# First two tiles of an FFN half-step together, a third of the tokens at a time, and a table for the steps of the norm

## The chip, the cores and the metric

The kernel runs on one core of a Trainium2 chip, as one program. The metric is its device time in microseconds (us). PE is TensorE, DVE VectorE, ACT ScalarE, POOL GpSimd, and SP the queue that issues most DMAs. Each engine works through its own queue of instructions in the order in which the program puts them, and waits at an instruction until what it needs has been signalled.

## What is computed

A diffusion backbone of two layers over 512 latent tokens and 256 context tokens of width 1024, in fp32. Each layer is a half-step FFN, a token mixing (two groups of attention heads with rotary positions, one output projection), and another half-step FFN. The last half-step is for the latent tokens alone.

```python
def swiglu_half_step(x, g, mod, j, w_up, w_down):
    h = modulate(rms_norm(x, g), mod[..., j, :], mod[..., j + 1, :])
    gt, up = jnp.split(h @ w_up, 2, axis=-1)
    return x + MACARON_W * mod[..., j + 2, :] * ((jax.nn.silu(gt) * up) @ w_down)

def reference(...):
    for l in range(DEPTH):
        x = swiglu_half_step(x, norm_g[l, 0], mod_x, 0, w_ffn_up[l, 0], w_ffn_down[l, 0])
        h_ctx = swiglu_half_step(h_ctx, norm_g[l, 0], mod_c, 0, w_ffn_up[l, 0], w_ffn_down[l, 0])
        ...
        x = x + mod_x[..., 5, :] * (jnp.concatenate([out_a, out_b], axis=-1) @ w_out[l])
        ...
        x = swiglu_half_step(x, norm_g[l, 2], mod_x, 6, w_ffn_up[l, 1], w_ffn_down[l, 1])
    return x
```

rms_norm divides each token by the root of its mean square; mod_x and mod_c come from a product of the conditioning vector with a large matrix, w_ada. FFN(l,j) below is half-step j of layer l: FFN(0,0), mixing, FFN(0,1), FFN(1,0), mixing, FFN(1,1).

## The kernel before

Tokens lie along the free dimension, channels on the 128 partitions; x is eight tiles of 128 channels. An fp32 product is three matmuls of rounded halves (`mm3`, L536 to L538): high x high, high x low, low x high. So everything that PE multiplies is split first: an activation into xh (ACT, L502) and xl (DVE, L503), a piece of 512 weight columns into whi (ACT, L144) and wlo (DVE, L145). Raw weights and wlo share a ring of 15 buffers, whi has six.

A half-step has 22 tiles f of 128 hidden channels, in five groups. The first PLAIN[l,j] tiles are plain: gate and up, eight k-steps, 48 matmuls for each range of tokens. The others take seven Strassen products of 12 matmuls each, over half the tokens. These need sums of the inputs, which `combine` makes (L518 to L528) once all tokens are normed, and sums of the weights (DVE, L131).

The norm of a half-step's input is begun at the end of the step before it. While the last output tiles of a range of tokens come out (a residual, L756; a square on ACT, L463; its sum into acc on DVE, L464), `background` sets up a generator `norm` for each range that is through. With FULL tokens the ranges are thirds of 256 tokens (latent, latent, context); in FFN(1,1) two halves of the latent tokens. `tick` moves all waiting generators one step; it is called after each output tile, and after every second k-step of a plain tile. A generator's steps are:

- the **root**: `rstd`, small matmuls that sum acc over the partitions (L483), a scaling on DVE (L485, the tile st), a power on POOL (L486);
- the **spread**: two transposes on PE that lay st over all partitions (L492);
- the **multiplies** (L498), xh (L502) and xl (L503), eight tiles of each.

Before, the root came at a generator's second tick and the spread at its fifth, everywhere. `flush` moves a generator on until its range is ready, if its products come before that.

The first tile f=0 goes a third at a time, so that the first third's products can run while the others are normed; from f=1 on a tile takes all tokens at once, hence needs all thirds. In FFN(0,0) f=0 is made at the start, ahead of this code.

A dot product of w_ada with the conditioning vector (`ada`, L449, on DVE; its weights adaw come by DMA) is put in wherever a tile begins, behind the last xl or split at that point (`self.anchor`). The mixing starts with projections (L880 to L882) per third, and builds tables for the rotation on POOL (L863, L870) from a load on SP (`ropet`, L859).

A scheduler turns the program's order into one queue for each engine; what it moves is shown under the change.

Of the kernel before, what the change touches and what calls it, by code (L numbers as in the profile page):

```python
# [28 lines left out]
PLAIN = {(0, 0): 3, (0, 1): 3, (1, 0): 3, (1, 1): 2}  # L29
# [39 lines left out]
class Weights:  # L69


    def __init__(self, k):
# [42 lines left out]
    def prepare(self, upto):  # L115
        while self.split < min(upto, len(self.order)):
# [45 lines left out]


# [6 lines left out]
class Kern:  # L170
# [336 lines left out]
    def combine(self, l, j, streams):  # L507
# [7 lines left out]
        for k in range(4):  # L515
# [9 lines left out]
            for d in (k, k + 4):  # L525
# [4 lines left out]
                x[d] = low  # L530


    def mm3(self, o, wh, wl, h, l, first, last, more=False):
# [4 lines left out]
        mm(o, wl, h, start=False, stop=last, skip_group_check=more)  # L538

    def ffn(self, l, j, first, streams, then):  # L540
# [16 lines left out]
        def hidden():  # L557
            hh = self.fp.tile([P, T], F32R, tag="hh", name="hh", bufs=5)
            return hh, self.fp.tile([P, T], F32, tag="hl", name="hr", bufs=6)

        def parted(hh, hr):
# [9 lines left out]
        def plain(f, item):  # L571

            done = begun and f == 0
            strs = first if f == 0 and not done else streams
            if done:
                o = self.first
            else:
                o = [[self.bank()[:, :s1 - s0] for _, s0, s1 in strs] for _ in range(2)]
                for sel in [[i] for i in range(len(strs))] if f == 0 else [range(len(strs))]:
                    if f == 0:  # L580
                        self.flush(strs[sel[0]][1])
                    for k in range(KD):
                        for gu in range(2):
                            w = [z[:, k % 4 * P:k % 4 * P + P] for z in ws.ready((item, k // 4 * 2 + gu))]
                            for i in sel:
# [704 lines left out]
```

## Time and profile before

| | us |
|---|---|
| median of three runs | 2694.51 |
| lowest and highest run | 2690.70, 2695.86 |
| the profiled execution | 2696.01 |
| its span, first to last instruction | 2693.9 |
| PE busy in the span | 2605.4 |
| DVE busy | 2091.5 |
| ACT busy | 1286.3 |
| POOL busy | 151.0 |
| mean granted clock of PE | 0.985 |

The durations of the next section are from the profiled execution. Rows of the timeline give the start in the span, the busy time, the engine, the line, and the instruction, written as output<-inputs; "x8" behind a row is eight in a row, and the bracket says how long the engine was idle before it and what ended that. Rows of a stretch give, for each engine, busy us and the number of instructions, then PE's granted clock (1.00 is full speed), the DMA share and GB/s. Rows of waits give the engine and what it waited for, us in all, how often, and the longest. PEld is the loading of weights into PE.

### The profile page before, as it was taken

Reading aid. Unit: us, or ns where it says so; the run is one execution under the profiler, and the core shown is the slowest. Engines: PE = TensorE matmul, PEld = TensorE weight load, DVE = VectorE, ACT = ScalarE, POOL = GpSimd, SP = SyncE. Lnnn points to the kernel's source line nnn. Section 1 sums busy time; section 2 is a strip of 40 time slices with the busy share of each in tenths; the row PEclk is TensorE's granted clock in tenths of the full one; section 3 lists DMA queues with packets and bytes.
Section 4 is the critical chain, followed back from the end, with each engine's and each line's share of the span. In section 5 each row is a group of like instructions: output and inputs, shape, how many; then the busy total and the mean of one; then the engine's idle time right before and its main releaser. Section 6 shows DMA issues by size and latency. Waiting matters only on the chain. (4 is left out here: it accounts for less than half of the span.)

```text
span 2693.9 us, 47286 instructions
## 1 busy us (share of the span) xinstructions
PE 2605.4 (97%) x17078; PEld 2471.4 (92%) x17078; DVE 2091.5 (78%) x4198; ACT 1286.3 (48%) x2671; POOL 151.0 (6%) x255
## 2 busy tenths in 40 slices
PE   7999999999999989999999899999998999799999
PEld 5999999989999879999999799999998998789998
DVE  6988888777889698788666877676767779787776
ACT  5343343445777553343344533432435677545543
POOL 0000000033210000000000000000014110000000
PEclk9999999999999989999999899999998999899999
DMA  8656646444235537466434365466345335555553
GB/s 325 198 185 204 214 130 211 124 134 142 90 93 174 171 112 225 147 198 210 154 96 147 113 189 193 132 200 199 108 145 152 98 105 167 164 167 177 159 165 116
DMA packets 306153, 433.22 MB, mean 161 GB/s; under 512 B 31440, under 2 KB 177232, under 8 KB 304464
## 3 DMA queue, kind: packets, MB, share of 16 engines
q1 hardware_dynamic: 305920, 430.21, 50.8%
q8 instruction: 134, 2.20, 0.3%
q14 instruction: 99, 0.81, 0.1%
HBM read 344.90 MB, written 88.34 MB: 161 GB/s over the span
## 5 line engine op out<-in xcount | busy, mean ns | idle before, releaser
L144 ACT CAST whi<-wraw 128x512 fp32r<-128x512 f32 (+1 forms) x644 | 389.3, 611 | 721.3 <-PE b L537 615.7
L145 DVE TENSOR_TENSOR wlo<-wraw,whi 128x512 fp32r<-128x512 f32 (+1 forms) x644 | 425.9, 674 | 62.9 <-ACT whi L144 43.6
L537 PE MATMUL b<-xl,whi 128*128 128x384 f32 (+2 forms) x1420 | 452.0, 320 | 2.0 <-DVE xl L503 2.0
L538 PE MATMUL b<-xh,wlo 128*128 128x384 f32 (+2 forms) x1420 | 448.9, 320 | 3.3 <-DVE wlo L145 3.3
L536 PE MATMUL b<-xh,whi 128*128 128x384 f32 (+2 forms) x1420 | 447.6, 320 | 3.3 <-ACT xh L502 3.1
L537 PE MATMUL b<-hl,whi 128*128 128x512 f32 (+1 forms) x1292 | 432.1, 337 | 0.0
L538 PE MATMUL b<-hh,wlo 128*128 128x512 f32 (+1 forms) x1292 | 427.8, 336 | 0.0
L536 PE MATMUL b<-hh,whi 128*128 128x512 f32 (+1 forms) x1292 | 413.5, 337 | 0.0
L537 PE MATMUL b<-x,whi 128*128 128x384 f32 (+1 forms) x1232 | 395.6, 322 | 0.0
L536 PE MATMUL b<-sh,whi 128*128 128x384 f32 (+1 forms) x1232 | 394.1, 322 | 0.9 <-ACT whi L144 0.5
L538 PE MATMUL b<-sh,wlo 128*128 128x384 f32 (+1 forms) x1232 | 388.0, 321 | 0.0
L449 DVE CUSTOM_DVE_ANT_0 junk<-adaw,sc,bada 128x1024 bf16<-128x1024 f32 x224 | 286.8, 1280 | 8.2 <-DMA adaw<-in_w_ada 6.1
L537 PEld LDWEIGHTS b<-xl,whi 128*128 128x128 f32 x1420 | 273.6, 193 | 8.1 <-DVE xl L503 2.6
L538 PEld LDWEIGHTS b<-xh,wlo 128*128 128x128 f32 x1420 | 272.2, 192 | 8.6 <-DVE wlo L145 3.7
L536 PEld LDWEIGHTS b<-xh,whi 128*128 128x128 f32 x1420 | 271.2, 193 | 9.5 <-ACT xh L502 3.6
L144 ACT CAST whi<-wt 128x512 fp32r<-128x512 f32 x231 | 144.1, 624 | 261.7 <-PE b L537 220.4
L537 PEld LDWEIGHTS b<-hl,whi 128*128 128x128 f32 x1292 | 244.7, 189 | 24.8
L538 PEld LDWEIGHTS b<-hh,wlo 128*128 128x128 f32 x1292 | 244.3, 189 | 25.1
L536 PEld LDWEIGHTS b<-hh,whi 128*128 128x128 f32 x1292 | 241.2, 189 | 26.2
L880 PE MATMUL mm<-whi,xh 128*128 128x256 f32 x800 | 231.8, 291 | 10.1 <-ACT raw L892 4.1
L536 PEld LDWEIGHTS b<-sh,whi 128*128 128x128 f32 x1232 | 231.9, 188 | 3.0 <-ACT whi L144 1.7
L537 PEld LDWEIGHTS b<-x,whi 128*128 128x128 f32 x1232 | 232.1, 188 | 1.5
(159 smaller groups left out, 4858.7 us busy)
## 6 DMA issues: line engine op xcount, KB each, us to landing
wraw<-in_w_up SPq DMA_DIRECT2D x352, 256.0 KB
adaw<-in_w_ada SPq DMA_DIRECT2D x130, 512.0 KB
wraw<-in_w_down SPq DMA_DIRECT2D x160, 256.0 KB
xsp<-x SPq DMA_DIRECT2D x140, 256.0 KB
xsp<-x SPq DMA_DIRECT2D x184, 128.0 KB
xl<-xsp SPq DMA_DIRECT2D x80, 256.0 KB
xh<-xsp SPq DMA_DIRECT2D x80, 256.0 KB
wraw<-in_w_in SPq DMA_DIRECT2D x72, 256.0 KB
```

The source lines that it names most:

```text
L144: k.nc.scalar.copy(hi[:, :w], raw[:, :w])
L145: k.nc.vector.tensor_tensor(out=lo[:, :w], in0=raw[:, :w], in1=hi[:, :w].bitcast(F32), op=ALU.subtract)
L449: nc.vector.tensor_tensor_reduce(out=junk, in0=w, in1=self.sc[:, cond, :], scale=1.0, scalar=self.bada[:, l, n:n + 1], op0=ALU.mult, op1=A ...
L536: mm(o, wh, h, start=first, stop=False, skip_group_check=more)
L537: mm(o, wh, l, start=False, stop=False, skip_group_check=more)
L538: mm(o, wl, h, start=False, stop=last, skip_group_check=more)
L880: nc.tensor.matmul(o, self.xh[:, k, ts], wh, start=k == 0, stop=False)
```

## The change

Three things change.

1. `PLAIN[(1,1)]` goes from 2 to 3, so FFN(1,1) has a third plain tile and one Strassen tile less.
2. In FFN(0,1), (1,0) and (1,1), `plain_two` makes f=0 and f=1 together: for each range of tokens first f=0's products, then f=1's. The weights of f=1 are now needed through all ranges; their high halves go into buffers for hidden activations (tag hh, five of them). `combine` becomes a generator: of its four steps, two come behind f=0's last range and two behind f=1's. FFN(0,0) goes on as it was.
3. `TICKS` gives the ticks of root and spread: for each range, by what comes next. "ffn" is a half-step in thirds, "mix" a mixing, "lat" the two halves of FFN(1,1). They were 2 and 5 for all.

```diff
-PLAIN = {(0, 0): 3, (0, 1): 3, (1, 0): 3, (1, 1): 2}
+PLAIN = {(0, 0): 3, (0, 1): 3, (1, 0): 3, (1, 1): 3}
...
+            if gi == 0 and (l, j) != (0, 0):
+                ws.guest.add(up[1])
...
-        hi = k.wsp.tile([P, PW], F32R, tag="whi", name="whi")
+        hi = k.hidden() if guest else k.wsp.tile([P, PW], F32R, tag="whi", name="whi")
...
+TICKS = {"ffn": [(3, 6), (3, 6), (5, 8)], "mix": [(3, 6), (3, 4), (2, 3)], "lat": [(2, 3), (3, 6)]}
...
-    def background(self, then, b, s0, s1):
-        self.bg.append((self.norm(*then, b, s0, s1), s0))
+    def background(self, then, i, n, b, s0, s1):
+
+        kind = "lat" if n == 2 else "mix" if then[1] == 1 else "ffn"
+        self.bg.append((self.norm(*then, b, s0, s1, *TICKS[kind][i]), s0))
...
-        yield
+        for _ in range(root - 1):
+            yield
         st = self.rstd(self.bank(), s0, s1)
-        yield
-        yield
-        yield
+        for _ in range(spread - root):
+            yield
         r = self.bank()
         self.spread(st, r[:, :s1 - s0])
...
+        def plain_part(item, s, o, ahead=AHEAD):
+
+            for k in range(KD):
+                for gu in range(2):
+                    w = [z[:, k % 4 * P:k % 4 * P + P] for z in ws.ready((item, k // 4 * 2 + gu), ahead)]
+                    for i, (b, s0, s1) in enumerate(s):
+                        self.mm3(o[gu][i], *w, self.xh[:, k, s0:s1], self.xl[:, k, s0:s1], k == 0, k == KD - 1)
+                if k % 2:
+                    self.tick()
...
+        def plain_two(items):
+
+            ws.after(items[1])
+            hr = [None, None]
+            for i, z in enumerate(first):
+                self.flush(z[1])
+                last = i == len(first) - 1
+                if last:
+                    ws.prepare(ws.index[items[1], 3] + 3)
+                    sums = self.combine(l, 2 * j, streams)
+                for f, item in enumerate(items):
+                    o = pair_of_banks([z])
+                    plain_part(item, [z], o, AHEAD if last and f else 0)
+                    hr[f] = hr[f] or product_place()
+                    gated(hr[f], [z], o)
+                    for _ in range(2 if last else 0):
+                        next(sums)
+            return [parted(h) for h in hr]
...
-                    hs.append(plain(f, items[f - f0]))
-                    if f == 0:
-                        self.combine(l, 2 * j, streams)
+                    if f == 0 and begun:
+                        hs.append(plain(0, self.first))
+                        list(self.combine(l, 2 * j, streams))
+                    elif f == 0:
+                        hs += plain_two(items[:2])
+                    elif f > 1 or begun:
+                        hs.append(plain(items[f - f0]))
```

The lines of the code before move down in the code after: the root L483, L485, L486 becomes L493, L495, L496, the spread L492 becomes L502, the multiplies and splits L498, L502, L503 become L508, L512, L513, acc L464 becomes L474, ada L449 becomes L459, wlo L145 becomes L147, and mm3 L547 to L549.

How the queues change at three places. First, PE's queue at the start of FFN(0,1), where the root of the last third stands (its tile acc is the sum of squares, xh and xl the split input; b are PSUM tiles). Before:

```order
L537 MATMUL b_11781<-xl_67,whi_11802 128x256
L538 MATMUL b_11781<-xh_66,wlo_11803 128x256
L483 MATMUL b_11871<-ones_69,acc_80 128x1 [waits DVE_49,PE_49]
L483 MATMUL b_11871<-ones_69,acc_80 128x1
L536 MATMUL b_11779<-xh_66,whi_11784 128x256 [waits Activation_49]
L537 MATMUL b_11779<-xl_67,whi_11784 128x256
L538 MATMUL b_11779<-xh_66,wlo_11785 128x256
```

After:

```order
L548 MATMUL b_11906<-xl_67,hh_11814 128x256
L549 MATMUL b_11906<-xh_66,wlo_11815 128x256
L493 MATMUL b_11920<-ones_69,acc_80 128x1 [waits DVE_49]
L493 MATMUL b_11920<-ones_69,acc_80 128x1
L502 MATMUL b_11962<-ident_68,st4_11923 128x128 [waits PE_49,Pool_49]
L502 MATMUL b_11962<-ident_68,st4_11923 128x128
L547 MATMUL b_11992<-xh_66,whi_11778 128x256 [waits Activation_49]
L548 MATMUL b_11992<-xl_67,whi_11778 128x256 [waits DVE_49]
```

Before, the root stood ahead of the second third's f=0 (from whi_11784 on), with f=0 of the first third ahead of it. After, f=1 of the first third (weights hh_11814) stands ahead of the root, and the last third's spread directly behind it, ahead of the second third's products (b_11992).

Second, DVE's queue at the same place, in which g_11746 is the last square of the last third, x and xl belong to the second third, and junk is a dot product of ada. Before:

```order
L503 SCALAR_TENSOR_TENSOR xl_67<-x_11244,mod_73,xh_66 128x256 [waits Activation_49]
L503 SCALAR_TENSOR_TENSOR xl_67<-x_11246,mod_73,xh_66 128x256 [waits Activation_49]
L449 ISA junk_11762,mod_73<-adaw_11754,sc_11749,bada_71 128x1024 [waits DVE_49]
L449 ISA mod_73 128x1
L464 TENSOR_TENSOR acc_80<-acc_80,g_11746 128x256 [waits DVE_49]
L449 ISA junk_11764,mod_73<-adaw_11754,sc_11749,bada_71 128x1024 [waits DVE_49]
L449 ISA mod_73 128x1
L485 TENSOR_SCALAR st4_11874<-b_11871 128x2 [waits PE_49,Pool_49]
```

After, the acc:

```order
L459 ISA junk_11758,mod_73<-adaw_11752,sc_11749,bada_71 128x1024 [waits DVE_49]
L459 ISA mod_73 128x1
L474 TENSOR_TENSOR acc_80<-acc_80,g_11746 128x256 [waits DVE_49,Activation_49]
L513 SCALAR_TENSOR_TENSOR xl_67<-x_11232,mod_73,xh_66 128x256 [waits Activation_49]
L513 SCALAR_TENSOR_TENSOR xl_67<-x_11234,mod_73,xh_66 128x256 [waits Activation_49]
```

and the scaling st:

```order
L513 SCALAR_TENSOR_TENSOR xl_67<-x_11244,mod_73,xh_66 128x256 [waits Activation_49]
L513 SCALAR_TENSOR_TENSOR xl_67<-x_11246,mod_73,xh_66 128x256 [waits Activation_49]
L459 ISA junk_11762,mod_73<-adaw_11754,sc_11749,bada_71 128x1024 [waits DVE_49]
L459 ISA mod_73 128x1
L495 TENSOR_SCALAR st4_11923<-b_11920 128x2 [waits PE_49,Pool_49]
```

The acc of g_11746 stood behind the second third's eight xl and a dot product; now it stands ahead of them. st stands behind them in both, with one dot product ahead of it where there were two.

Third, DVE's queue at the start of FFN(1,1): the residuals (x<-b), the accs and the dot products. Before, ahead of the first half's root:

```order
L756 SCALAR_TENSOR_TENSOR x_27008<-b_27240,mod_73,x_27008 128x256 [waits DMAHW5_49,PE_49]
L449 ISA junk_27351,mod_73<-adaw_27345,sc_27336,bada_71 128x1024 [waits DMAHW3_49]
L449 ISA mod_73 128x1
L464 TENSOR_TENSOR acc_80<-acc_80,g_27219 128x256 [waits DVE_49,Activation_49]
L756 SCALAR_TENSOR_TENSOR x_27002<-b_27258,mod_73,x_27002 128x256 [waits PE_49]
L145 TENSOR_TENSOR wlo_27401<-wraw_27082,whi_27400 128x512 [waits Activation_49]
L756 SCALAR_TENSOR_TENSOR x_27004<-b_27276,mod_73,x_27004 128x256 [waits PE_49]
L449 ISA junk_27355,mod_73<-adaw_27349,sc_27336,bada_71 128x1024 [waits DMAHW5_49,DVE_49]
L449 ISA mod_73 128x1
L464 TENSOR_TENSOR acc_80<-acc_80,g_27237 128x256 [waits DVE_49]
```

After, around the second half's st (L495):

```order
L513 SCALAR_TENSOR_TENSOR xl_67<-x_27112,mod_73,xh_66 128x256 [waits Activation_49]
L459 ISA junk_27474,mod_73<-adaw_27470,sc_27467,bada_71 128x1024
L459 ISA mod_73 128x1
L474 TENSOR_TENSOR acc_80<-acc_80,g_27464 128x256 [waits Activation_49]
L459 ISA junk_27478,mod_73<-adaw_27472,sc_27467,bada_71 128x1024 [waits DVE_49]
L459 ISA mod_73 128x1
L459 ISA junk_27482,mod_73<-adaw_27476,sc_27467,bada_71 128x1024 [waits DMAHW2_49,DVE_49]
L459 ISA mod_73 128x1
L495 TENSOR_SCALAR st4_27577<-b_27574 128x2 [waits PE_49]
L459 ISA junk_27486,mod_73<-adaw_27480,sc_27467,bada_71 128x1024 [waits DMAHW3_49,DVE_49]
```

Before, four dot products stood among the residuals and accs of the first half, the last two of them here. After, they stand behind the first half's xl, three ahead of the second half's st, of which the third waits for its load.

More of the change, by code (lines that the diff above doesn't have):

```diff
@@ L124, in prepare @@
                 raw = self.raw(i, c)
-            self.done[key] = self.halves(raw, w)
+            self.done[key] = self.halves(raw, w, i in self.guest)
             self.split += 1
@@ L464, in square, with norm @@
             nc.vector.tensor_tensor(out=self.acc[:, c0:c0 + 256], in0=self.acc[:, c0:c0 + 256], in1=sq, op=ALU.add)
-    def norm(self, l, j, cond, s0, s1):
-        yield
+    def norm(self, l, j, cond, s0, s1, root, spread):
+        for _ in range(root - 1):
+            yield
         st = self.rstd(self.bank(), s0, s1)
-        yield
-        yield
-        yield
+        for _ in range(spread - root):
+            yield
         r = self.bank()
@@ L538, in mm3, with hidden @@
         mm(o, wl, h, start=False, stop=last, skip_group_check=more)
+    def hidden(self):
+        return self.fp.tile([P, T], F32R, tag="hh", name="hh", bufs=5)
     def ffn(self, l, j, first, streams, then):
@@ L555, in spread, with product_place, parted @@
             state[1] = want
[L557 to L561, printed above, removed]
+        def product_place():
+            return self.fp.tile([P, T], F32, tag="hl", name="hr", bufs=6)
+        def parted(hr):
+            hh = self.hidden()
             hl = self.fp.tile([P, T], F32R, tag="hl", name="hl", bufs=6)
@@ L569, in temp @@
             return self.fp.tile([P, w], F32, tag=tag, name=tag, bufs=bufs)
[L571 to L579, printed above, removed]
-                    if f == 0:
[L581 to L585, printed above, removed]
-                                s0, s1 = strs[i][1:]
-                                self.mm3(o[gu][i], *w, self.xh[:, k, s0:s1], self.xl[:, k, s0:s1],
-                                         k == 0, k == KD - 1)
-                        if k % 2:
-                            self.tick()
-            hh, hr = hidden()
-            for i, (b, s0, s1) in enumerate(strs):
+        def plain_part(item, s, o, ahead=AHEAD):
[6 more added lines that the diff above has]
+                    self.tick()
@@ L593, in plain, with gated, pair_of_banks @@
+        def gated(hr, s, o):
+            for i, (b, s0, s1) in enumerate(s):
                 nc.scalar.activation(out=hr[:, s0:s1], in_=o[0][i], func=AF.Silu)
                 nc.vector.tensor_tensor(out=hr[:, s0:s1], in0=o[1][i], in1=hr[:, s0:s1], op=ALU.mult)
-            return parted(hh, hr)
+        def pair_of_banks(s):
+            return [[self.bank()[:, :s1 - s0] for _, s0, s1 in s] for _ in range(2)]
+        def plain(item, o=None):
+            if o is None:
+                o = pair_of_banks(streams)
+                plain_part(item, streams, o)
+            hr = product_place()
+            gated(hr, streams, o)
+            return parted(hr)
@@ L745, in ffn @@
             if final and then:
-                for z in strs:
+                for i, z in enumerate(strs):
                     for d in range(4, KD):
@@ L1204, in out_final @@
                 if us[-1] == 3:
[L1205 removed]
+                    self.background(then, z, len(streams), b, s0, s1)
 def _constants():
```

21 lines of the change are left out of this document (10 added, 11 removed).

## Prediction

> **What bounds the kernel now.** I read the page first, then the waits of TensorE (PE), then the stretches of 25 us in which PE falls short, and last the timeline there.
>
> ```profile
> span 2693.9 us, 47286 instructions
> PE 2605.4 (97%) x17078; PEld 2471.4 (92%) x17078; DVE 2091.5 (78%) x4198; ACT 1286.3 (48%) x2671; POOL 151.0 (6%) x255
> ...
> PE b L483 <- DVE acc L464: 27.5, 5, 10.4
> PE b L538 <- DVE wlo L145: 3.3, 2, 2.1
> ```
>
> PE is the bound: it is busy for 2605.4 us and idle for about 88. The change hardly touches the matmuls, so it can only win back idle time and time at a reduced clock. The largest wait is 27.5 us in five places: PE stands at the root of a norm (L483), because DVE has not yet added up the squares (L464). Where these places are, the stretches show (PE busy, PEld, DVE, ACT, POOL, then the granted clock, DMA share and GB/s).
>
> ```profile
> 560.00:585.00 25.00, 19.18 (x130) 17.82 (x129) 18.32 (x47) 8.65 (x23) 6.94 (x19) 0.86 0.22 66
> 950.00:975.00 25.00, 14.59 (x95) 14.06 (x95) 24.05 (x54) 12.45 (x27) 1.74 (x1) 0.73 0.32 102
> 1475.00:1500.00 25.00, 13.93 (x93) 13.41 (x92) 22.46 (x50) 12.07 (x25) 3.07 (x2) 0.73 0.39 121
> 2300.00:2325.00 25.00, 20.36 (x172) 20.17 (x171) 19.92 (x44) 12.63 (x23) 0.00 (x0) 0.91 0.81 272
> 2325.00:2350.00 25.00, 17.81 (x96) 16.11 (x97) 16.55 (x42) 12.40 (x27) 1.39 (x2) 0.70 0.21 65
> ```
>
> They are the starts of the half-steps FFN(0,1) near 950, FFN(1,0) near 1480 and FFN(1,1) near 2320; the first mixing, near 560, loses less, and the second repeats it near 2010. DVE is nearly full at these starts (24.05 of 25 near 950): it sets the pace, and PE waits for what stands last in DVE's queue.
>
> **FFN(0,1) and FFN(1,0).** The chain before, from the timelines of DVE, PE and POOL:
>
> ```profile
> 953.87 3.22 DVE L498 SCALAR_TENSOR_TENSOR x<-x,amul,b 128x256 f32<-128x256 f32 x8
> 958.55 0.42 DVE L464 TENSOR_TENSOR acc<-acc,g 128x256 f32<-128x256 f32 x1
> 958.88 3.25 DVE L503 SCALAR_TENSOR_TENSOR xl<-x,mod,xh 128x256 fp32r<-128x256 f32 x8
> 963.25 0.42 DVE L464 TENSOR_TENSOR acc<-acc,g 128x256 f32<-128x256 f32 x1
> 963.82 0.98 PE L483 MATMUL b<-ones,acc 128*128 128x1 f32 x4 [10.41 <-DVE acc L464]
> 964.91 0.16 DVE L485 TENSOR_SCALAR st<-b 128x2 f32<-128x2 f32 x1
> 965.15 1.74 POOL L486 TENSOR_TENSOR st<-st,nhalf 128x2 f32<-128x2 f32 x1 [16.94 <-DVE st L485]
> ...
> 1481.61 0.28 PE L536 MATMUL b<-xh,whi 128*128 128x256 f32 x1
> 1482.55 0.28 PE L538 MATMUL b<-xh,wlo 128*128 128x256 f32 x1
> 1492.74 0.99 PE L483 MATMUL b<-ones,acc 128*128 128x1 f32 x4 [9.90 <-DVE acc L464]
> ...
> L145 DVE TENSOR_TENSOR wlo<-wraw,whi 128x512 fp32r<-128x512 f32 (+1 forms) x644 | 425.9, 674 | 62.9 <-ACT whi L144 43.6
> L449 DVE CUSTOM_DVE_ANT_0 junk<-adaw,sc,bada 128x1024 bf16<-128x1024 f32 x224 | 286.8, 1280 | 8.2 <-DMA adaw<-in_w_ada 6.1
> ```
>
> PE is through with the first third (f=0 alone) and stands for 10.41 us at the root of the last third, whose last acc comes at 963.25, behind eight xl and a dot product of ada. The second third's products stand behind that root, although their xh and xl are coming. From 1481.61 to 1482.55 PE starts nine matmuls, one every 0.94 / 8 = 0.1175 us; I use this for 256 columns.
>
> After the change two things differ in PE's queue. The first third now has f=1 behind f=0: 86 matmuls stand ahead of the root where 50 stood, so 36 more are done in the idle time, 36 x 0.1175 = 4.2 us. And the spread (two transposes that wait for POOL) follows the root directly, ahead of all products of the second third. DVE's new order pulls the last acc ahead of the eight xl: after the multiplies at 953.87 (3.2) only a wlo (0.7) and a dot product (1.3) precede it, so it comes at about 959, and the root is no longer late. But st (L485) stands behind eight xl (3.2), a product of the size of an acc (0.4) and one more dot product (1.3): at about 963.8. POOL's power takes 1.74 and starts 0.24 later, so the spread comes at 965.8, and the second third begins there, where it began after the root's 0.8, at 964.6, before. **So the wait is not removed but renamed**, from acc to st, and 1.2 us of the 4.2 go back: gain 3.0. FFN(1,0) has the same rows 529 us later (9.90 for 10.41) and the same new order: 3.0 again. Bounds of each: 4.5, if the power takes 0.70 (a row below shows that) and DVE gains a little; 1, if DVE is 2 us later than I count. An idle stretch of 5 us or more stays in each place, so the clock falls as before:
>
> ```profile
> 964.00:968.00 4.00, 4.00 (x19) 4.00 (x20) 3.61 (x7) 0.41 (x1) 1.74 (x1) 0.50 0.41 131
> 968.00:972.00 4.00, 4.00 (x30) 4.00 (x30) 3.45 (x7) 0.43 (x2) 0.00 (x0) 0.80 0.37 131
> ```
>
> From 964 to about 970 the matmuls run at 0.50, which costs half of 6 us: some 3 us a spell, unchanged here.
>
> **The mixings.** The last third's power waits in POOL's queue behind the rope tables, whose load waits on SP:
>
> ```profile
> 563.16 0.42 SPq L859 DMA_DIRECT2D ropet<-in_ropet  x1
> 567.44 0.91 POOL L863 TENSOR_TENSOR rt<-ropet,grow 128x256 f32<-128x256 f32 x1 [9.43 <-DMA xs<-xsp]
> 570.93 0.15 DVE L485 TENSOR_SCALAR st<-b 128x2 f32<-128x2 f32 x1
> 573.68 0.70 POOL L486 TENSOR_TENSOR st<-st,nhalf 128x2 f32<-128x2 f32 x1
> 574.43 0.43 PE L492 MATMUL b<-ident,st 128*128 128x128 f32 x2 [1.01 <-POOL st L486]
> 576.00:578.00 2.00, 0.70 (x4) 0.51 (x4) 2.00 (x6) 2.00 (x6) 0.00 (x0) 0.77 0.00 0
> 580.00:582.00 2.00, 2.00 (x11) 2.00 (x11) 1.29 (x4) 0.00 (x0) 0.00 (x0) 0.50 0.00 0
> ```
>
> st is ready at 570.93, and its power starts at 573.68. The table moves the spread ahead of 24 products of the second third, which then fill PE (24 x 0.1175 = 2.8 us) while DVE multiplies and splits the last third (3.2 each). But 6.2 us of rope work still stand ahead of the power. Their load stands behind a weight whose buffer DVE frees a place or two earlier, which I put at 1.2 us. So the spread would come at 573.2; the fill works for its 2.8 us; and the last third's root now waits some 1.3 us for its acc. 1.2 + 2.8 - 1.3 is 2.7 at best; since part of the fill only stood elsewhere before, I take 2.0 us for each mixing, 4 together. Bounds of each: 0, if the fill wins nothing, and 5, if the half clock after 576 goes with it.
>
> The Trainium skill, "TensorE: Matmul & The Clock Gate", section "HAM oscillation — how this bites in real kernels", has the abstract rule "no PE-idle gaps >~3.4µs". The rows above differ: the one wait shown there is 1.01 us, and yet the clock is 0.50 at 580, behind a stretch in which PE was busy for 0.70 of 2.00; the busy share tells, not one gap. By the rule a start with short gaps alone would run at full clock.
>
> **FFN(1,1).** Here are only two thirds (halves of the latent tokens), and they wait in series:
>
> ```profile
> 2310.42 1.29 DVE L449 CUSTOM_DVE_ANT_0 junk<-adaw,sc,bada 128x1024 bf16<-128x1024 f32 x1 [1.46 <-DMA xsp<-x]
> 2323.95 1.01 PE L483 MATMUL b<-ones,acc 128*128 128x1 f32 x4 [4.64 <-DVE acc L464]
> 2331.38 0.70 PE L536 MATMUL b<-xh,whi 128*128 128x256 f32 x2 [1.83 <-ACT xh L502]
> 2334.52 1.02 PE L483 MATMUL b<-ones,acc 128*128 128x1 f32 x4 [2.44 <-DVE acc L464]
> 2343.77 0.97 PE L536 MATMUL b<-xh,whi 128*128 128x256 f32 x4 [1.30 <-ACT xh L502]
> 2346.37 0.58 PE L537 MATMUL b<-xl,whi 128*128 128x256 f32 x1 [1.62 <-DVE xl L503]
> 2376.13 0.58 PE L538 MATMUL b<-xh,wlo 128*128 128x256 f32 x1 [2.13 <-DVE wlo L145]
> ```
>
> The five waits up to 2346.37 sum to 11.8 us. PE resumes three times (2324, 2334.5, 2346.4) at half clock, by the mean clocks of 0.91 and 0.70 above for about 4, 4 and 5.5 us; half of that is 6.8. Lost in all: 18.6 us.
>
> After the change, step by step. Four dot products of ada leave the stretch before the first root (four of 1.28 and 1.46 of waiting are 6.6 us, more than the 4.64), so the root follows PE at 2319.3. The spread now stands one tile (12 matmuls, 1.4 us) behind it; a residual and an acc (0.4 each), st and a power of 0.70 do not quite fit in: idle 0.9. The next tile ends near 2323, but the eight multiplies began only at 2321.5, and a wlo, an acc and a residual stand ahead of xl: xl near 2326.3, idle 3.3 us. From there f=0 and f=1 of the first half are 96 matmuls, 11.3 us, and beside them DVE does xl, three dot products, st and the multiplies of the second half, whose spread comes near 2337 and whose xl near 2341: idle about 1.8. In all 6.0 us idle where 11.8 stood, and I charge half clock for 8 us, 4.0 where 6.8 stood. Gain 18.6 - 10.0 = 8.6.
>
> The third plain tile lies between these halves and the first Strassen product: 48 matmuls of 512 columns, 96 x 0.1175 = 11 us of cover more for DVE's splits, so that the wait at 2376.13 goes: 2.1, and some 2 for a spell behind it like the others. Its price: 24576 columns in place of 7 x 12 x 256 = 21504, so 3072 / 256 x 0.1175 = 1.4 us. Sum: 8.6 + 4.1 - 1.4, about 11. Bounds: 3, if the late wait stays and the second half's chain ends as late as now, and 18, if nearly all that is lost is won back.
>
> **The rest.** f=1 in thirds has as many columns as before, and its weights are split once, as before. I cost it at nothing; if each of the 48 added matmuls cost 0.01 us, it would be 0.5 in a half-step. The Strassen sums in steps are the same work on DVE, covered by f=2. FFN(0,0) keeps its tiles.
>
> **Sum.** 3.0 + 3.0 + 4 + 11 = 21 us. The profiled execution took 2696.0 (the span of 2693.9 and 2.1 around it), 1.5 above the median of the runs, 2694.5. 2696.0 - 21 = 2675.0; on the median's footing **2673.5 us, which I predict**. The bounds add to 1 + 1 + 0 + 3 = 5 and 4.5 + 4.5 + 10 + 18 = 37.
>
> **Rivals.**
>
> The wait only changes its name. Each spread arrives as late as the acc did, since DVE has 24.05 of 25 us of work near 950 and its work is not less. Then FFN(0,1), FFN(1,0) and the mixings gain nothing, and FFN(1,1) its 3: 2691.5. For it: DVE's and POOL's rows. Against it: 36 matmuls and four dot products do move.
>
> Loads come late: slower. f=0 and f=1 together hold eight low halves in a ring of 15 buffers through all thirds, where four were held, so the raw weights for f=2 and the Strassen sums find four buffers fewer. If they can be loaded only when the last third has freed them, PE stands there for a load (4.3 us, as from the issue at 563.16 to its use at 567.44), a cast and a wlo (0.7 each): 5.7, and a spell of 3 behind it, 8.7 in each of three half-steps, 26 in all: 2700. It is slower than before once that wait with its spell exceeds 7 us. Against it: the first buffers for f=2 are those that the work ahead of the half-step frees, and near 950 the DMA share is 0.32.
>
> The clock follows gaps, not shares: the 4.0 of FFN(1,1) are not lost, 2669.5. Against it stands the row at 580. This is what the rule quoted above from the Trainium skill would make of it.
>
> **How the numbers follow.** The forecast with its bounds 0.76, the clock by gaps 0.05, the renamed wait 0.12, late loads 0.07. 0.2% of 2694.5 is 5.4 us, about what a measurement of this kernel tells from no change; the renamed wait falls inside it, the rest of the first two cases is faster. Faster 0.81, same 0.12, slower 0.07. The range takes in the forecast's bounds, and the renamed wait: 2657 to 2692.
>
> **What would show it.** PE's waits for acc at L493 come to under 8 us in all. In FFN(0,1) and FFN(1,0) PE waits instead at L502 for POOL's st, 5 to 8 us each. In FFN(1,1) no wait of PE is over 4 us, and none for wlo near 2370. In the mixings the last third's spread comes 1 to 3 us earlier. Wrong would be a wait for a wlo or a raw weight at f=2 or behind it, or a last spread behind POOL's rope work as late as now.

## The result and the profile after

| | before | after |
|---|---|---|
| median, us | 2695.19 | 2680.60 |
| lowest and highest run, us | 2690.70, 2696.72 | 2679.13, 2681.60 |
| the profiled execution, us | 2696.01 | 2681.60 |
| runs | 4 | 4 |

The changed kernel takes 0.9948 of the time before, with a 95% interval of 0.9931 to 0.9965: 14.6 us less, where 21 were forecast. The time lies inside the range. A later repeat, measured beside more runs of before, gave 2678.28 us and 0.9941 (0.9929 to 0.9953).

First the page of after, and its waits of PE (us in all, how often, the longest).

```profile
span 2679.8 us, 47467 instructions
PE 2602.0 (97%) x17186; PEld 2475.5 (92%) x17186; DVE 2085.4 (78%) x4190; ACT 1281.0 (48%) x2667; POOL 149.9 (6%) x255
...
PE b L502 <- POOL st L496: 22.8, 8, 5.6
PE b L548 <- DVE xl L513: 8.8, 4, 3.0
PE mm L917 <- ACT raw L929: 6.2, 6, 3.8
PE b L493 <- DVE acc L474: 2.1, 3, 1.4
```

PE's 27.5 us of waiting for acc have become 2.1, and instead PE waits 22.8 us for st, the root's own output, at the spread. Two of the eight waits, 5.6 and 4.7 us, are in FFN(0,1) and FFN(1,0); the four in the mixings sum to 11.4 and the two in FFN(1,1) to 1.2. The clock and the busy time at the same stretches:

```profile
560.00:585.00 25.00, 20.37 (x140) 19.85 (x141) 19.52 (x49) 8.97 (x23) 7.71 (x20) 0.86 0.22 59
950.00:975.00 25.00, 19.39 (x148) 19.31 (x148) 24.96 (x55) 15.19 (x34) 1.72 (x1) 0.83 0.28 85
1475.00:1500.00 25.00, 18.90 (x130) 18.64 (x129) 24.96 (x57) 15.63 (x35) 1.72 (x1) 0.74 0.33 99
2300.00:2325.00 25.00, 23.49 (x195) 22.88 (x194) 18.59 (x44) 16.04 (x32) 1.07 (x1) 1.00 0.71 223
2325.00:2350.00 25.00, 20.64 (x154) 19.79 (x155) 21.01 (x49) 12.59 (x28) 0.69 (x1) 0.93 0.43 125
2350.00:2375.00 25.00, 25.00 (x160) 22.42 (x159) 25.00 (x49) 15.04 (x29) 0.00 (x0) 1.00 0.59 181
```

PE is fuller in every one (the row of before from 2350 stands further down). At FFN(1,1) the clock has gone from 0.91 and 0.70 to 1.00 and 0.93; at FFN(1,0) it is 0.74, where it was 0.73.

To see which stage won and which lost, I take the start of one and the same matmul in two profiles: the last down matmul of a half-step, and the first and the last matmul of the attention with v (`pv`). The difference in length of a stage between two such marks is its gain (minus is faster, us; "after again" is the profile of the repeat).

| stage | forecast | after | after again |
|---|---|---|---|
| to the end of FFN(0,0) | 0 | +1.2 | +0.3 |
| first mixing, up to the first pv | -2.0 | -1.6 | -2.1 |
| its attention | 0 | -0.4 | -0.4 |
| FFN(0,1) | -3.0 | -2.8 | -1.9 |
| FFN(1,0) | -3.0 | -1.7 | -2.8 |
| second mixing, up to the first pv | -2.0 | **+5.2** | **+5.1** |
| its attention | 0 | -0.6 | -0.6 |
| FFN(1,1) | -11 | -13.3 | -13.5 |

One stage is clearly on the wrong side: the second mixing, by 7 us, and that is as much as is missing from the forecast; the smaller deviations cancel. Each of these lengths comes from one execution: in two runs below that leave the rows of the second mixing as they were, it is 1.8 and 2.4 us shorter than in before, so a difference of 2 us in one stage says little by itself. Two questions were left for the chip: which part of the change costs the second mixing its 5 us, and which part brings FFN(1,1) its 13. A third came from the row of 22.8 us: whether the spread's place is what PE pays for in FFN(0,1) and FFN(1,0).

### The profile page after: what moved, and what is told of

It reads as the page before. It is cut to its first block, busy times and chain, and to the rows that moved or that the text cites. A ratio compares the mean times of both kernels' runs of the same rounds, so it can differ in the third digit from the quotient of the medians.

```text
span 2679.8 us, 47467 instructions
## 1 busy us (share of the span) xinstructions
PE 2602.0 (97%) x17186; PEld 2475.5 (92%) x17186; DVE 2085.4 (78%) x4190; ACT 1281.0 (48%) x2667; POOL 149.9 (6%) x255
## 5 line engine op out<-in xcount | busy, mean ns | idle before, releaser
L146 ACT CAST whi<-wraw 128x512 fp32r<-128x512 f32 (+1 forms) x632 | 381.6, 609 | 718.8 <-PE b L548 616.4
L147 DVE TENSOR_TENSOR wlo<-wraw,whi 128x512 fp32r<-128x512 f32 (+1 forms) x632 | 417.6, 673 | 66.0 <-ACT whi L146 48.2
L549 PE MATMUL b<-xh,wlo 128*128 128x384 f32 (+2 forms) x1472 | 456.6, 314 | 0.4 <-DVE wlo L147 0.4
L548 PE MATMUL b<-xl,whi 128*128 128x384 f32 (+2 forms) x1344 | 425.4, 318 | 8.8 <-DVE xl L513 8.8
L549 PE MATMUL b<-hh,wlo 128*128 128x512 f32 (+1 forms) x1292 | 427.6, 336 | 0.0
L547 PE MATMUL b<-xh,whi 128*128 128x384 f32 (+2 forms) x1344 | 422.2, 319 | 0.9 <-ACT hr L663 0.6
L547 PE MATMUL b<-hh,whi 128*128 128x512 f32 (+1 forms) x1292 | 413.9, 337 | 0.0
L547 PE MATMUL b<-sh,whi 128*128 128x384 f32 (+1 forms) x1216 | 389.3, 322 | 0.3
L549 PE MATMUL b<-sh,wlo 128*128 128x384 f32 (+1 forms) x1216 | 382.8, 322 | 0.0
L459 DVE CUSTOM_DVE_ANT_0 junk<-adaw,sc,bada 128x1024 bf16<-128x1024 f32 x224 | 286.4, 1279 | 13.5 <-DMA adaw<-in_w_ada 12.8
L549 PEld LDWEIGHTS b<-xh,wlo 128*128 128x128 f32 x1472 | 279.5, 191 | 4.1 <-DVE wlo L147 0.7
L548 PEld LDWEIGHTS b<-xl,whi 128*128 128x128 f32 x1344 | 256.9, 191 | 13.9 <-DVE xl L513 9.8
L549 PEld LDWEIGHTS b<-hh,wlo 128*128 128x128 f32 x1292 | 244.2, 189 | 25.2
L547 PEld LDWEIGHTS b<-hh,whi 128*128 128x128 f32 x1292 | 241.2, 189 | 26.1
L547 PEld LDWEIGHTS b<-xh,whi 128*128 128x128 f32 x1344 | 255.4, 192 | 5.5 <-ACT hr L663 0.8
L917 PE MATMUL mm<-whi,xh 128*128 128x256 f32 x800 | 233.6, 293 | 6.5 <-ACT raw L929 6.2
L547 PEld LDWEIGHTS b<-sh,whi 128*128 128x128 f32 x1216 | 228.7, 188 | 2.3 <-ACT whi L146 0.9
```

The lines of the kernel that those rows point to most:

```text
L146: k.nc.scalar.copy(hi[:, :w], raw[:, :w])
L147: k.nc.vector.tensor_tensor(out=lo[:, :w], in0=raw[:, :w], in1=hi[:, :w].bitcast(F32), op=ALU.subtract)
L459: nc.vector.tensor_tensor_reduce(out=junk, in0=w, in1=self.sc[:, cond, :], scale=1.0, scalar=self.bada[:, l, n:n + 1], op0=ALU.mult, op1=A ...
L547: mm(o, wh, h, start=first, stop=False, skip_group_check=more)
L548: mm(o, wh, l, start=False, stop=False, skip_group_check=more)
L917: nc.tensor.matmul(o, self.xh[:, k, ts], wh, start=k == 0, stop=False)
```

## The experiments

Each is timed beside runs of the kernel before on the same chip. Ratios are to before, with the 95% interval.

| run | median, us | runs | ratio |
|---|---|---|---|
| old ticks for all (e1) | 2683.07 | 5 | 0.9959 (0.9942 to 0.9976) |
| table alone (e2) | 2692.32 | 10 | 0.9992 (0.9983 to 1.0002) |
| after with two plain tiles (e3) | 2687.36 | 10 | 0.9976 (0.9966 to 0.9985) |
| third plain tile alone (e5) | 2692.54 | 10 | 0.9992 (0.9982 to 1.0002) |
| old ticks in the mixings (e4) | 2672.82 | 4 | 0.9919 (0.9904 to 0.9933) |
| last spread later (e6) | 2663.82 | 4 | 0.9884 (0.9867 to 0.9900) |
| e6, and old ticks in the second mixing (e7) | 2660.71 | 4 | 0.9874 (0.9859 to 0.9888) |
| only the last third early in mixings (e8) | 2678.41 | 4 | 0.9938 (0.9923 to 0.9953) |
| after again (e10) | 2678.28 | 5 | 0.9941 (0.9929 to 0.9953) |
| old ticks in FFN(1,1) (e11) | 2683.50 | 6 | 0.9959 (0.9945 to 0.9973) |
| several rows together (e9) | 2680.56 | 5 | 0.9944 (0.9931 to 0.9958) |
| after, v cast on DVE (e12) | 2680.16 | 5 | 0.9948 (0.9935 to 0.9962) |

The stages of the first seven, against before as above (us):

| stage | e1 | e2 | e3 | e5 | e4 | e6 | e7 |
|---|---|---|---|---|---|---|---|
| first mixing | -0.1 | -2.1 | -1.8 | -0.4 | +0.2 | -1.5 | -1.9 |
| FFN(0,1) | -0.6 | +1.2 | -1.7 | 0.0 | -2.2 | -9.0 | -7.7 |
| FFN(1,0) | +0.1 | -3.0 | -3.1 | +0.2 | -2.9 | -8.6 | -9.2 |
| second mixing | -2.4 | +3.2 | +4.9 | -1.8 | -3.6 | +1.3 | -1.6 |
| FFN(1,1) | -12.2 | -2.2 | -3.3 | -0.1 | -13.7 | -13.1 | -15.1 |

### Which part pays in FFN(1,1)

The first of four runs is after with the old root and spread everywhere.

```diff
-TICKS = {"ffn": [(3, 6), (3, 6), (5, 8)], "mix": [(3, 6), (3, 4), (2, 3)], "lat": [(2, 3), (3, 6)]}
+TICKS = {"ffn": [(2, 5)] * 3, "mix": [(2, 5)] * 3, "lat": [(2, 5)] * 2}
```

> The changed kernel with root and spread back at ticks 2 and 5 everywhere: two tiles together and the third plain tile alone. Theory A (the table carries most of the gain of FFN(1,1), by taking four dot products out of DVE's way; the pair needs it): FFN(1,1) gains 3 to 5 us, FFN(0,1) and FFN(1,0) 0 to 1 each, the mixings stand as before the change; in all 2689 to 2692. Theory B (the pair of tiles is the cover that matters, the table is a detail): FFN(1,1) gains 9 or more and the total is 2681 to 2685.

The second is before with the table and nothing else: no pair, two plain tiles.

```diff
+TICKS = {"ffn": [(3, 6), (3, 6), (5, 8)], "mix": [(3, 6), (3, 4), (2, 3)], "lat": [(2, 3), (3, 6)]}
...
-    def background(self, then, b, s0, s1):
+    def background(self, then, i, n, b, s0, s1):
```

> The kernel before with the table alone: f=0 alone in thirds, PLAIN of FFN(1,1) at 2. Theory A: FFN(1,1) gains 4 to 7 us though nothing covers its second half; the first mixing gains 2 and the second loses 4, as in the changed kernel; FFN(0,1) and FFN(1,0) gain nothing or lose up to 3 each, since the last third's spread now stands behind 96 matmuls only; in all 2690 to 2696. Theory B: FFN(1,1) gains at most 1, and the total is 2697 or more.

The third is after without the third plain tile.

```diff
-PLAIN = {(0, 0): 3, (0, 1): 3, (1, 0): 3, (1, 1): 3}
+PLAIN = {(0, 0): 3, (0, 1): 3, (1, 0): 3, (1, 1): 2}
```

> The changed kernel with PLAIN of FFN(1,1) back at 2: no third plain tile. If the third tile is worth its cover, the wait for a wlo at the first Strassen products comes back (2 us and a spell at half clock behind it), less 1.4 us of matmul columns saved: 2.5 to 3 us slower than the changed kernel, 2683 to 2684. If the pair alone covers DVE's splits, it is 1.4 us faster than the changed kernel, 2679.

The fourth is before with the third plain tile and nothing else.

```diff
-PLAIN = {(0, 0): 3, (0, 1): 3, (1, 0): 3, (1, 1): 2}
+PLAIN = {(0, 0): 3, (0, 1): 3, (1, 0): 3, (1, 1): 3}
```

> The kernel before with PLAIN of FFN(1,1) at 3 and nothing else. If the wait for a wlo at 2376 and the spell behind it go for 1.4 us of columns, 2.5 to 3 us faster than before: 2692. If the splits are late anyway, 1.4 us slower than before: 2696.5.

Of FFN(1,1)'s 13.3 us the pair and the third tile without the table keep 12.2 (e1). The table alone has 2.2, the third tile alone 0.1, and the pair with the table but without the third tile 3.3. Neither half does much by itself; together they bring nearly all. (The run of the pair without both, table and third tile, was not made.) The first run came out as its Theory B had it, and the second's gain in FFN(1,1) lies between its two theories. The third is slower than both of its expectations. The fourth has the total of its first expectation, but by luck: the profile has its gain in the mixings, not in FFN(1,1). The profile of e3 tells why the pair needs the third tile. Here are PE's waits there, behind the pair of tiles (timeline):

```profile
2361.86 0.39 PE L548 MATMUL b<-x,whi 128*128 128x256 f32 x1 [2.86 <-DVE x L538]
2366.08 0.58 PE L548 MATMUL b<-x,whi 128*128 128x256 f32 x1 [3.24 <-DVE x L538]
```

In e3 the Strassen products come right behind the pair, and `combine` has not made their sums: its DVE part can start only when the last half is split, about 2341, and now has no third plain tile beside it. What the pair wins at the roots is lost here. In after the third tile stands in this place, and in the stretch from 2350 to 2375 PE is busy for all 25.00 us. The same stretch in before and in e3:

```profile
2350.00:2375.00 25.00, 23.50 (x150) 21.14 (x148) 24.96 (x51) 16.59 (x33) 0.00 (x0) 0.96 0.38 120
2350.00:2375.00 25.00, 17.59 (x127) 16.49 (x126) 25.00 (x48) 13.27 (x27) 0.00 (x0) 0.86 0.33 108
```

In e5, without the pair, PE's waits in the half-step fall from 14.7 to 13.0 us (sums of the timeline): the 2.13 for wlo and a 0.50 ahead of it go, and three new waits of 0.5 to 0.8 come. The added columns, at an estimated 1.4, take nearly all of that, and the stage gains 0.1.

In e1, PE's waits for acc (4 of them, 22.6 us) are back, all but one of them outside FFN(1,1): the wait at its first root is 2.1 us there. So in FFN(1,1) the table is worth 13.3 - 12.2 = 1.1 us by this run. By the run that puts only this row back, it is more:

```diff
-... "lat": [(2, 3), (3, 6)]}
+... "lat": [(2, 5), (2, 5)]}
```

> The changed kernel with only the row of FFN(1,1) back at ticks 2 and 5. If the table is worth about 1 us in FFN(1,1), as the run with old ticks everywhere says (12.2 won there, against 13.3 in the changed kernel), 2681 to 2683. If the dot products that the table moves out of DVE's way are worth the 4 us of the prediction, 2684 or more.

Measured: 2683.50 us, FFN(1,1) -9.4 us against before, so 3.9 us for the row. Its waits of PE (same columns as above):

```profile
PE b L502 <- POOL st L496: 21.4, 7, 5.1
PE b L493 <- DVE acc L474: 9.9, 5, 4.7
```

The waits for acc are 7.8 us longer than in after; 6.7 us of them are at the two roots of FFN(1,1), which come too early again. Two runs thus give the row 1.1 and 3.9 us. The profiled execution of e11 was the fastest of its six, 5 us below their median, so this is loose; which value is nearer is not shown.

### The second mixing

In this run only the row for mixings goes back.

```diff
-... "mix": [(3, 6), (3, 4), (2, 3)], ...
+... "mix": [(2, 5)] * 3, ...
```

> The changed kernel with root and spread of the two mixings back at ticks 2 and 5; the other two rows of the table stay. Theory C (the earlier spreads lengthen the start of the second mixing by 5 to 7 us, from the end of FFN(1,0) to its first attention products, and shorten that of the first by 1.6): the second mixing's stretch is 78 to 80 us again (85.4 in the changed kernel), and the total is 2675 to 2677. Theory D (what FFN(0,1) and FFN(1,0) win is taken back there whatever the table says, since the keys and values go through DRAM and the load ends at its own time): the stretch stays at 84 to 85 us, and the total is 2682.

Measured: 2672.82 us, 5 to 8 below the two medians of after; the second mixing is at -3.6 where it was at +5.2 (76.7 us from FFN(1,0)'s last matmul to the first pv; 80.3 before, 85.4 after). The first mixing loses its gain, -1.6 to +0.2. So in this pair of runs the row brings the first mixing 2 us and costs the second 9; the total is below what either theory expected. In e6 and e7 of the next section, which differ in this row for the second mixing alone, it costs 2.9.

Where most of the 9 are: in after the first 336 matmuls of the stage take 49.0 us, a little less than before (49.7; both counted from FFN(1,0)'s last matmul). The next 48 take 16.1 us, where before takes 12.6 and e4 10.0. There the projections' results go to DRAM (scr), and v, k and q are loaded back from it. First the timeline of after in that place, from SP, ACT, DVE and PE:

```profile
2043.21 0.37 SPq L981 DMA_DIRECT2D vn<-scr  x1
2046.18 0.51 ACT L1039 CAST v<-vn 128x384 fp32r<-128x384 f32 x1 [3.14 <-DMA vn<-scr]
2046.72 0.56 DVE L1041 TENSOR_TENSOR v<-vn,v 128x384 fp32r<-128x384 f32 x1 [2.41 <-ACT v L1039]
2048.08 0.37 ACT L929 COPY raw<-mm 128x256 f32<-128x256 f32 x1 [0.67 <-DVE t L957]
2052.78 0.58 PE L917 MATMUL mm<-whi,xh 128*128 128x256 f32 x1 [3.81 <-ACT raw L929]
```

And the same place in e4:

```profile
2044.35 0.51 ACT L1039 CAST v<-vn 128x384 fp32r<-128x384 f32 x1 [3.66 <-DMA vn<-scr]
2044.90 0.56 DVE L1041 TENSOR_TENSOR v<-vn,v 128x384 fp32r<-128x384 f32 x1 [0.70 <-ACT v L1039]
2050.43 0.38 PE L917 MATMUL mm<-whi,xh 128*128 128x256 f32 x1 [1.14 <-ACT raw L929]
```

ACT stands at a cast for a load from DRAM (3.14 us in after, and 3.66 in e4, so its length alone does not make the loss), and the copies raw<-mm that empty PE's banks stand behind it. In turn they need a buffer raw, of which there are two, and DVE frees it (L957) behind its own part of v (L1041), at which it stands too: 2.41 us in after, 0.70 in e4. In after that L1041 comes one projection earlier in DVE's queue: 7 of the products st precede it, where before and in e4 8 do. PE waits longest at L917: 3.81 and 1.14 us.

Two runs were meant to narrow it. In one only the last third keeps its early root and spread:

```diff
-... "mix": [(3, 6), (3, 4), (2, 3)], ...
+... "mix": [(2, 5), (2, 5), (2, 3)], ...
```

> The changed kernel with the mixings' first two spreads back at ticks 2 and 5, and only the last third's spread early (2, 3). If the wait of 3.2 us for the second spread, at the start of the mixing, is what lengthens the second mixing, its stretch is 78 to 80 us and the first mixing keeps its 1.6: 2673 to 2676. If it is the regrouping of the pieces behind the last spread, the stretch stays near 84 and the total at 2680.

Measured: 2678.41 us; the first mixing -3.5, the best of all, the second +0.8 (81.1 us), with a wait for raw of 4.1. The last third's entry alone keeps the long wait. Neither expectation came true: the stretch is shorter than 84 us, and the total higher than 2676. In the other, the cast leaves ACT:

```diff
-            nc.scalar.copy(v[:, :, 0], vn)
+            nc.vector.tensor_copy(out=v[:, :, 0], in_=vn)
```

> After, with the cast v<-vn of the second head group (L1039) on DVE in place of ACT; nothing else. In the second mixing of after, ACT stands 3.14 us at this cast for a load, the copies raw<-mm that free TensorE's banks stand behind it, and TensorE waits 3.81 us for one of them. Theory: ACT's stand is what makes the seven kernels with the new row for mixings lose 3 to 5 us here. Then TensorE's waits for raw fall from 6.2 us in all to under 3, the stretch from FFN(1,0)'s last matmul to the first pv matmul goes from 85.4 us to 80 to 82, and the kernel to 2674 to 2677 us. Rival: the loads come late, and it doesn't matter which engine stands for them; DVE, which is 8.28 of 10 us busy there, then stands instead and holds the products that the later stores need. Then the stretch stays at 84 to 87 us, TensorE waits for qn or kh in place of raw, and the time is 2678 to 2682.

Measured: 2680.16 us, the time of after. In the profile (timeline of DVE and PE):

```profile
2042.47 0.36 DVE L1039 CAST v<-vn 128x384 fp32r<-128x384 f32 x1 [2.53 <-DMA vn<-scr]
2050.65 0.58 PE L917 MATMUL mm<-whi,xh 128*128 128x256 f32 x1 [5.75 <-ACT raw L929]
```

My theory that ACT's stand makes the wait falls: DVE stands for the load instead (2.53 us), ACT's copies wait for DVE, and PE's wait grows to 5.75. The rival was right about the time and that the wait follows to the other engine, but not in that PE would wait for qn or kh in its place. The stretch was 81.3 us in this profile, though that execution was the fastest of five (2676.64), so it says little.

So it is shown that the row for mixings costs the second mixing of after 3 to 9 us, and that PE's wait for raw behind the load of vn is longer with it. It is not shown what in the order decides its length. In all eight profiles with the new row or its last entry in this mixing, PE's longest wait for raw is 3.12 to 5.75 us, and the stretch 81.1 to 85.4. Before and in four of the five others the wait is 1.00 to 1.86, and the stretch 76.7 to 80.3. But the fifth of these, the run of several rows below, has the old row in the second mixing and yet 3.72 and 84.4. So the old row does not suffice: what else is in the queues decides too.

The wait is also not the whole loss. With the same row and the same queues up to this place, e11's stretch was 81.3 and after's 85.4, though PE's waits in it sum to 12.8 and 13.0 us. What differs is the clock. Here are 25 us from about the same point of the stage in before, after, e4 and e11:

```profile
2050.00:2075.00 25.00, 20.48 (x142) 18.97 (x142) 19.69 (x52) 11.69 (x26) 15.13 (x19) 0.86 0.70 211
2045.00:2070.00 25.00, 18.07 (x103) 16.85 (x103) 17.20 (x47) 9.83 (x24) 13.38 (x17) 0.73 0.61 172
2046.00:2071.00 25.00, 20.62 (x163) 19.36 (x163) 20.15 (x53) 13.31 (x30) 14.02 (x20) 1.00 0.67 204
2043.00:2068.00 25.00, 17.88 (x121) 16.55 (x120) 19.43 (x52) 11.13 (x26) 13.24 (x19) 0.86 0.65 189
```

PE is busy for 18.07 us in after and for 17.88 in e11, but does 103 matmuls at a clock of 0.73 there and 121 at 0.86 here. In e4 the waits in the stage sum to 9.3 us and this stretch runs at 1.00. Of the 8.7 us between after and e4 the waits are 3.7; the other 5.0 go with the lower clock (at most 0.27 x 25 = 6.75 us here). Why the same queues got a different clock, and why the first mixing does not lose, stays open.

### The place of the spread

The waits of 5.61 and 4.72 us for st say that PE reaches the spread too early in FFN(0,1) and FFN(1,0). In this run the last third's spread comes two ticks later, behind the second third's f=0 (48 matmuls).

```diff
-TICKS = {"ffn": [(3, 6), (3, 6), (5, 8)], ...
+TICKS = {"ffn": [(3, 6), (3, 6), (5, 10)], ...
```

> The changed kernel with the spread of the last third at tick 10 in place of 8 before FFN(0,1) and FFN(1,0), so that it stands behind f=0 of the second third (48 matmuls) and ahead of f=1. If PE's 5.6 and 4.7 us at the spread are a matter of its place in the queue alone, they go, with the half clock behind them: 3 to 6 us less in each of the two, 2669 to 2675. If DVE's work is what ends last, the wait comes back at the last third's xh or xl: 0 to 1 each, 2679 to 2681.

Measured: 2663.82 us, 14 to 17 below the two medians of after and below both expected ranges. The waits of PE, two stretches and PE's spread in FFN(0,1):

```profile
PE b L502 <- POOL st L496: 10.9, 6, 3.2
```

```profile
950.00:975.00 25.00, 24.79 (x210) 24.34 (x210) 24.96 (x58) 16.73 (x37) 1.72 (x1) 1.00 0.25 79
1475.00:1500.00 25.00, 23.38 (x183) 22.77 (x182) 24.06 (x55) 17.38 (x39) 1.73 (x1) 0.93 0.28 86
```

```profile
964.83 0.43 PE L502 MATMUL b<-ident,st 128*128 128x128 f32 x2 [0.21 <-POOL st L496]
```

The spread waits 0.21 us where it waited 5.61 (the row of after stands in the section on the prediction), PE is busy for 24.79 of 25 us at full clock, and DVE is as full as in after (24.96). FFN(0,1) gains 9.0 us against before and FFN(1,0) 8.6, where after has 2.8 and 1.7. So DVE was not the bound there: there was enough work for PE, and one small group of instructions in PE's queue kept it from that work. The pair is part of this: in e2, without it, the last spread also stands some 46 matmuls behind its root, yet FFN(0,1) loses 1.2 us and FFN(1,0) gains 3.0.

Then the same with the old row in the second mixing alone.

```diff
-        kind = "lat" if n == 2 else "mix" if then[1] == 1 else "ffn"
+        kind = "lat" if n == 2 else ("old" if then[0] else "mix") if then[1] == 1 else "ffn"
```

> The changed kernel with the last third's spread at tick 10 before the two FFNs, and the second mixing alone back at ticks 2 and 5. Theory C with the spread's place: the gains of both add up, 2663 to 2669, the fastest. Theory D: as with the later spread alone.

Measured: 2660.71 us (2657.59 to 2663.55), the fastest of all. The intervals of this and the run before overlap, but the stages fit: second mixing 78.7 us for 81.6. A row of its page and one of its waits:

```profile
PE 2592.9 (98%) x17186; PEld 2465.9 (93%) x17186; DVE 2082.7 (78%) x4190; ACT 1281.0 (48%) x2667; POOL 147.5 (6%) x255
...
PE b L502 <- POOL st L496: 7.2, 4, 3.2
```

### Several rows together, and after again

Last, a table put together from rows that looked better each by itself.

```diff
-TICKS = {"ffn": [(3, 6), (3, 6), (5, 8)], "mix": [(3, 6), (3, 4), (2, 3)], "lat": [(2, 3), (3, 6)]}
+TICKS = {"ffn": [(2, 5), (3, 6), (5, 10)], "mix": [(2, 5), (2, 5), (2, 3)], "old": [(2, 5)] * 3, "lat": [(1, 2), (3, 6)]}
```

> The parts that won, together: before the two FFNs the first range at ticks 2 and 5, the last third's spread at tick 10; before the first mixing only the last spread early; before the second mixing the old ticks; before FFN(1,1) root and spread of the first half one tick earlier. If the parts add up, 2655 to 2660, faster than all others; if the earlier first spread only brings a wait at its own place, as in the mixing, 2661 or more.

Measured: 2680.56 us, 20 above e7: a miss. From its waits of PE:

```profile
PE b L549 <- DVE wlo L147: 10.6, 6, 3.2
PE b L493 <- DVE acc L474: 6.8, 5, 4.0
```

FFN(0,1) and FFN(1,0) keep 3.9 and 4.0 us of gain, half of what e7 has. With the first spread earlier the scheduler orders the queues anew: the last spread then stands 24 matmuls into the second third, not 48, and PE waits for weights' low halves that e7 hardly waits for. That is about half of the 20 us. The second mixing, though its row is e7's, takes 84.4 us for e7's 78.7, and FFN(1,1), with another row, gains 12.1 for e7's 15.1; these two were not followed. Rows that are good one by one don't add.

> The changed kernel itself once more, beside the next two on the same chip: 2679 to 2682 if its first four runs stand for it.

Measured: 2678.28 us, 2.3 below the first measurement of after and just under the expected 2679 to 2682, and the second mixing again at +5.1 us. The loss there is no chance of one execution.

## Why the prediction was right, and where it was wrong

**FFN(0,1) and FFN(1,0): right, chain and size.** Here is that chain in after, from PE, DVE and POOL, with the end of FFN(1,0)'s:

```profile
958.55 0.42 DVE L474 TENSOR_TENSOR acc<-acc,g 128x256 f32<-128x256 f32 x1
959.49 0.50 PE L493 MATMUL b<-ones,acc 128*128 128x1 f32 x4
963.59 0.15 DVE L495 TENSOR_SCALAR st<-b 128x2 f32<-128x2 f32 x1
963.82 1.72 POOL L496 TENSOR_TENSOR st<-st,nhalf 128x2 f32<-128x2 f32 x1 [14.89 <-DVE st L495]
965.60 0.69 PE L502 MATMUL b<-ident,st 128*128 128x128 f32 x2 [5.61 <-POOL st L496]
...
1492.29 0.69 PE L502 MATMUL b<-ident,st 128*128 128x128 f32 x2 [4.72 <-POOL st L496]
```

I had the last acc at about 959 (958.55), st at 963.8 (963.59) and the spread at 965.8 (965.60). The stage begins 0.9 us earlier in after (by its mark, the last pv), so counted from there each of the three came 0.4 to 0.7 us later than I had it. The wait was renamed, as forecast: 5.61 and 4.72 us for POOL's st. A second wait, which I did not have, stands ahead of it in FFN(0,1): 2.54 us for xl at 947.83, where before has 0.36. The gains of 2.8 and 1.7 (repeat: 1.9 and 2.8) stand for 3.0 each, and the spell at half clock stays:

```profile
964.00:968.00 4.00, 2.40 (x11) 2.41 (x12) 3.96 (x9) 2.12 (x5) 1.54 (x1) 0.50 0.43 131
968.00:972.00 4.00, 4.00 (x32) 4.00 (x32) 4.00 (x10) 2.96 (x8) 0.00 (x0) 0.88 0.11 17
```

What I had not asked is how much stood behind the spread: e6 shows 6 to 7 us more in each half-step, by its place alone.

**FFN(1,1): right, a little more than forecast.** Its waits of PE in after are

```profile
2321.85 0.43 PE L502 MATMUL b<-ident,st 128*128 128x128 f32 x2 [0.70 <-POOL st L496]
2323.99 0.50 PE L547 MATMUL b<-xh,whi 128*128 128x256 f32 x2 [0.30 <-ACT xh L512]
2327.48 0.58 PE L548 MATMUL b<-xl,whi 128*128 128x256 f32 x1 [2.99 <-DVE xl L513]
2338.57 0.43 PE L502 MATMUL b<-ident,st 128*128 128x128 f32 x2 [0.47 <-POOL st L496]
2343.02 0.39 PE L548 MATMUL b<-xl,whi 128*128 128x256 f32 x1 [1.40 <-DVE xl L513]
```

and sum to 5.9 us; 6.0 were worked out, with 3.3 us before xl (2.99) as the longest. The wait for wlo near 2376 is gone. I charged 4.0 us for half clock; a clock of 0.93 over 25 us is 0.07 x 25 = 1.75. That difference of 2.25 is about what 13.3 exceeds 11 by. My split of the 11 into 8.6 for the pair and table and 2.7 for the third tile was a split in name only: e3 and e5 show 3.3 and 0.1 for them alone, and e1 12.2 for pair and tile without the table. "The Strassen sums in steps are the same work on DVE, covered by f=2" was the sentence that held the answer: without f=2 they cost 6.1 us.

**The first mixing: size right, step wrong.** I had the last spread 1.2 us earlier. It came at 576.21 in after (574.43 before), 0.6 us later once the 1.2 us that the kernel was late at the end of FFN(0,0) are taken off. That is one of my own signs of being wrong: the last spread is as late as before, behind POOL's rope work. The rope load was issued 0.7 us earlier in the stage (563.60), but POOL began its work on it at 569.31, 5.7 us behind the issue where I had counted 4.3; what ended that wait was not followed. Its waits at the spreads:

```profile
561.41 0.43 PE L502 MATMUL b<-ident,st 128*128 128x128 f32 x2 [3.19 <-POOL st L496]
576.21 0.50 PE L502 MATMUL b<-ident,st 128*128 128x128 f32 x2 [2.95 <-POOL st L496]
```

and the ten us behind the last spread:

```profile
577.00:587.00 10.00, 10.00 (x76) 10.00 (x76) 8.38 (x24) 6.07 (x17) 0.51 (x2) 0.86 0.17 47
```

The fill did its work: behind the spread PE is busy for 10.00 of 10 us at a clock of 0.86. Before, it was busy for 8.43 of 10 at 0.66, in the same place:

```profile
576.00:586.00 10.00, 8.43 (x48) 8.27 (x49) 7.25 (x22) 5.34 (x16) 0.22 (x2) 0.66 0.16 44
```

Against it stands a new wait of 3.19 us at an earlier spread, which I hadn't seen. The ten us around it, before and after:

```profile
556.00:566.00 10.00, 9.04 (x66) 7.88 (x66) 9.90 (x24) 4.76 (x13) 1.47 (x1) 1.00 0.56 161
557.00:567.00 10.00, 6.81 (x45) 6.57 (x44) 10.00 (x27) 5.86 (x14) 0.87 (x1) 0.83 0.64 163
```

So 21 matmuls are lost there of the 28 that are won behind the last spread. That the sum is near 2.0 is partly luck.

**The second mixing: wrong, the step that failed.** "I take 2.0 us for each mixing" assumed that the second repeats the first, and that nothing behind the projections cares for their order; my lower bound was 0. The chip gave +5.2. The step looked at the norm alone; the stage has a second dependence, out to DRAM and back, and what I moved went past it in the queues of ACT and DVE. The runs of the section above show that the row makes this loss in after, as a longer wait for raw and a lower clock around it, and leave open what in the order does it, as one run has the loss with the old row too. With -2.0 replaced by +5.2 the forecast of 21 becomes 14, as measured, since the other deviations cancel.

**The rivals.** The renamed wait was real in name, but not over the whole: most of the time came from FFN(1,1). Late loads did not appear: PE has no wait for a raw weight at the third tile or behind it, and its waits for wlo in after come to 0.4 us (1.8 in the repeat). If the clock went by gaps alone, all 4.0 us in FFN(1,1) would have been saved; 2.25 were, with no wait above 2.99.

## What to carry to other kernels

Before a wait is moved, look at what stands behind the waiting instruction in its queue: here two small transposes, put 48 matmuls later, were worth as much as the whole change. A part that makes a wait short must be counted with the cover that the next wait needs, as the pair (with the table) and the third tile were worth 0 to 3 us apart and 12 together. A stage that looks like an earlier one has to be followed to its last dependence before its gain is taken over.

## What the hardware showed

The same power on POOL, 128x2, took 1.72 us at 963.82 (after 14.89 us of idle POOL), 0.87 at 560.49 (after 10.97) and 0.69 at 575.46 (directly behind other work of POOL). I had used 0.70 and 1.74 as a price for a place; what decides between them was not tried.

The clock went to 0.86 in the first mixing of after, with waits of 3.19 and 2.95 us as PE's longest there, and to 0.93 in FFN(1,1) with none above 2.99. The Trainium skill, "TensorE: Matmul & The Clock Gate", section "HAM oscillation — how this bites in real kernels", has "no PE-idle gaps >~3.4µs" as the rule for a kernel that keeps its clock. The rows differ from it: shorter waits, of about 3 us, were followed by a lower clock here too.
